# Attention scores: q loaded once and k in both orders of its halves, instead of q in both orders and k once

## The chip, the cores and the metric

The kernel runs on one core of a Trainium2 chip. The metric is the device time of one execution in microseconds (us); times here are medians of several runs. A profile of one execution comes with it, with the span from the first to the last instruction, each engine's instructions and each DMA.

The engines are named as in the profile: PE is the matmul engine TensorE (PEld its weight loads), DVE is VectorE, ACT is ScalarE, POOL is GpSimd, and SP is SyncE, which here only issues DMAs. Every engine runs its own instructions in order.

## The reference, cut to what matters

One transformer layer in float32 over two sequences, a prompt of 1024 tokens and a sample of 512, each with 16 meta tokens ahead. Half of the mixer is grouped-query attention (8 q heads of 64 that share 2 k and v heads), the other half differential attention (4 heads, two softmax maps each).

```
n  = rms_norm(h);  qa, ka, va, qb, kb, vb = split(n @ w_in)
# group A, 8 heads, k and v shared by four
s  = qa . ka / 8 ;  oa = softmax(s) @ va
# group B, 4 heads, maps 0 and 1
s  = qb[c] . kb[c] / 8 ;  a = softmax(s[0]) - lam * softmax(s[1]) ;  ob = rms_norm(a @ vb)
h  = h + concat(oa, ob) @ w_out
n  = rms_norm(h)
h  = h + (gelu(conv3(n @ w_gate)) * (n @ w_up)) @ w_down
y  = rms_norm(h)[16:]
```

q and k of group A are normalised per head, and q and k of both groups are rotated (rotary position).

## The kernel before, in words

**Precision.** A float32 operand is split into hi (rounded to the fast matmul type float32r) and lo (the rest). A dense product is three matmuls: hi hi, hi lo, lo hi (`mm3`, L129 to L131; `split` is L123 and L124). For scores the 64 rows of a head's q stand on the 128 rows of TensorE twice: hi over lo. A k tile holds k's hi over lo. One matmul of q (hi over lo) with k gives hi hi + lo lo, and a second one of q in the other order (lo over hi) gives the two mixed products. Both go to the same PSUM tile (L401 and L402).

**Where q and k come from.** `finish` in the projection writes hi and lo of q and k to DRAM, q as hi, lo, hi so that two neighbours can be read in either order (L237 to L247). `stacked` (L366) reads two neighbours of one head into a 128-row tile, on SP's queue. Its source has four levels: (2 orders x 2 halves) x 32 rows x tokens.

**Tiles.** s is 0 for the prompt (n = 1040 tokens, three pieces of 348 columns for PSUM, so 4 pad columns filled by a second small `stacked`) and 1 for the sample (n = 528, two pieces of 264, no pad). `load_q` takes up to 512 queries, in two tiles, `load_k` a whole k. Pools hold the tiles: `kp` for k, `qp` for q, `pp` for p, and so on; a tile can be loaded again when its last reader is done. A softmax takes up to 128 queries: two matmuls per piece, the scaled copy with its row minimum (L405, DVE), the exponential (L408, ACT), transposes (L422, PE, 128x128), their hi and lo (L123, L124), and the product with v (L432 to L446). In group A the reciprocals of the row sums go through DRAM (`rT`, stored at L454, loaded back at L470); SP waits for the store before it can issue that load. Each of the 4 differential heads has two k (m = 0, 1), a v and three (s = 0) or two (s = 1) blocks of queries; p0 is combined with p1 on POOL (L526, L528). `halo` collects the last meta token's query of four heads.

**Order of the program.** Projection of s = 1 (up to 160 us of the profile); attention of s = 1 merged with the projection of s = 0 (up to about 550 us); attention of s = 0 merged with `mixer_out` and `conv_glu` of s = 1 (up to about 1400 us); `mixer_out` of s = 0 with the rest of that; `conv_glu` of s = 0 (to the end). `merge` interleaves two generators by the work that they report; a scheduler that works with expected durations then sets the order on each engine for the whole program, DMA queues too. So the order moves when a tile's number of buffers or an instruction changes. `mixer_out` (s = 1) begins with h loaded from `oT` (L608, SP), which attention (s = 1) has stored; then its hi (L123, ACT) and the first `mm3`. Weights w_f are loaded on ACT's queue, 512 KB at a time, and split into w_hi and w_lo (L150 on POOL or ACT).

Of the kernel before, what the change touches and what calls it, by code (L numbers as in the profile page):

```python
# [12 lines left out]
F32 = mybir.dt.float32  # L13
F32R = mybir.dt.float32r
# [6 lines left out]
P = 128  # L21
D = 1024
KT = D // P
NMETA = 16
HD = 64
# [10 lines left out]
QA, KA, VA, QB, KB, VB = 0, 4, 5, 6, 10, 14  # L36
# [67 lines left out]
def pool(ctx, g, name, bufs, side):  # L104
    return ctx.enter_context(g.tc.tile_pool(name=name, bufs=bufs, side=side, reuse_waits="tile"))
# [51 lines left out]
def projection(ctx, g, s, side, tag, tag2):  # L157

    nc, tc = g.nc, g.tc
    n = SEQS[s] + NMETA  # L160
# [18 lines left out]
    first = load_weight(g, g.w_in[KA])  # L179

    with tc.tile_pool(name=f"ps{s}", bufs=2, side=side, reuse_waits="tile") as sp:
# [4 lines left out]
        for k in range(KT):  # L186
            x = sp.tile([P, n], F32, name="x", tag="x", bufs=2 if s == 0 else 8)
# [12 lines left out]
        c0, cw = chunks[0]  # L200
        first_ps = g.psum.tile(P, cw, tag)
        dense(g, first_ps, first, xhi, xlo, c0, cw)
        for i, (c0, cw) in enumerate(chunks):
            if s == 1:
                ps = ms[i]
            else:
                ps = g.psum.tile(P, cw, tag2)
# [29 lines left out]
    def finish(y, hn, dst, keys, c0, cw):  # L237

        if hn is not None:
            nc.vector.tensor_tensor(out=y, in0=y, in1=hn[:, None, :].broadcast_to(list(y.shape)), op=ALU.mult)  # L240
        hi = tmp(bp, "hi", y.shape[1], cw, 2, F32R)
        lo = y.bitcast(F32R)
        split(g, hi, lo, y, nc.gpsimd)
        for i, part in enumerate((hi, lo) if keys else (hi, lo, hi)):
            to = dst[i, :, :, c0:c0 + cw]
            to = to.rearrange("x p n -> p x n") if y.shape[1] == 2 else to.rearrange("x p n -> (x p) n")[:, None]
            nc.sync.dma_start(out=to, in_=part.bitcast(F32))  # L247
# [101 lines left out]
def attention(ctx, g, s, side):  # L349
    nc, tc = g.nc, g.tc  # L350
    N = SEQS[s]
    n = N + NMETA

    nch = -(-n // 512)
    kw = -(-n // nch)
    kw += kw % 2
    ne = nch * kw
    nf = n // P
    sp = pool(ctx, g, f"as{s}", 8, side)
    kp = pool(ctx, g, f"ak{s}", 4, side)  # L360
    qp = pool(ctx, g, f"aq{s}", 3 if s == 0 else 2, side)
    vp = pool(ctx, g, f"av{s}", 2, side)
    pp = pool(ctx, g, f"ap{s}", 9 if s == 0 else 6, side)
    ptp = pool(ctx, g, f"apt{s}", 3 if s == 0 else 2, side)
    op = pool(ctx, g, f"ao{s}", 2, side)
    def stacked(tl, j, m, first, c0, cw):  # L366

        src = g.ka[s] if j == KA else g.qk[s][PAIRS.index(j)]
        parts = src[first:first + 2].rearrange("p x (m r) n -> (p x) m r n", r=32)
        nc.sync.dma_start(out=tl.bitcast(F32), in_=parts[:, m, :, c0:c0 + cw])  # L370

    def load_q(j, m, c0, cw):
        out = []
        for first in range(2):
            q = qp.tile([P, 512], F32R, name="q", tag=f"q{first}")[:, :cw]
            stacked(q, j, m, first, c0, cw)
            out.append(q)
        return out

    def load_k(j, m):  # L380
        k = kp.tile([P, ne], F32R, name="k", tag="k")
        stacked(k[:, :n], j, m, 0, 0, n)
        if ne > n:
            stacked(k[:, n:], j, m, 0, 0, ne - n)
        return k

    def load_v(i, w, c0):
        v = vp.tile([P, nf, 2 * P], F32R, name="v", tag="v")[:, :, :w]
# [4 lines left out]

    def softmax(q, k, l):

        M = q[0].shape[-1]
        p = pp.tile([P, ne], F32, name="p", tag="p")[:M]
        ps = g.psum.wide(M, nch, kw)
        for i in range(nch):
            kc = k[:, i * kw:(i + 1) * kw]  # L400
            nc.tensor.matmul(ps[:, i], lhsT=q[0], rhs=kc, start=True, stop=False)  # L401
            g.mark = nc.tensor.matmul(ps[:, i], lhsT=q[1], rhs=kc, start=False, stop=True).ins  # L402

        nm = sp.tile([P, 1], F32, name="nm", tag="nm")[:M]
        nc.vector.tensor_scalar(out=p.rearrange("p (i w) -> p i w", i=nch), in0=ps, scalar1=-HD ** -0.5, scalar2=3.0e38,  # L405
                                op0=ALU.mult, op1=ALU.min, accum_out=nm)
        p = p[:, :n]
        nc.scalar.activation(p, p, AF.Exp, bias=nm, scale=-1.0, accum_out=l)  # L408
        return p
# [46 lines left out]
    def finish_a(o, W):  # L456
        low = op.tile([P, 512], F32, name="o_low", tag="w1", bufs=1)[:HD, :W]
        nc.scalar.copy(low, o[HD:P, :])
        oa = op.tile([P, 512], F32, name="o_a", tag="o", bufs=3)[:HD, :W]
        nc.vector.tensor_tensor(out=oa, in0=o[0:HD, :], in1=low, op=ALU.add)  # L460
        return oa

# [18 lines left out]
    for kv in range(2):  # L481
        k = load_k(KA, kv)
        v = load_v(0, P, kv * P)
        for i in range(4):
            h = kv * 4 + i
            for b in range(nblk):
                q = load_q(QA + 2 * kv, i, NMETA + 512 * b, 512)
                load_r()
                pl = []
                l = sp.tile([P, 4], F32, name="l_a", tag="l_a", bufs=3)  # L490
                for t in range(4):
                    pl.append(softmax([x[:, t * P:(t + 1) * P] for x in q], k, l[:, t:t + 1]))
                    yield 2 * n
                cols = slice(1 + 512 * b, 513 + 512 * b)
                reciprocals(l, g.rT[s][h, cols].rearrange("(t p) -> p t", p=P))
                o, W = yield from weighted_v(pl, v, False)
                oa = finish_a(o, W)
                store_a()
                late.append((oa, g.rT[s][h:h + 1, cols], g.oT[s][h * HD:(h + 1) * HD, cols]))
        halo = [sp.tile([P, 8], F32R, name="halo", tag=f"halo{f}", bufs=2) for f in range(2)]  # L500
        for i in range(4):
            for f in range(2):
                stacked(halo[f][:, 2 * i:2 * i + 2], QA + 2 * kv, i, f, NMETA - 2, 2)
        l = sp.tile([P, 4], F32, name="l_a", tag="l_a", bufs=3)[:8, 0:1]
        load_r()
        p = softmax(halo, k, l)
        r = sp.tile([P, 4], F32, name="r_a", tag="r_a", bufs=3)[:8, 0:1]
        nc.vector.reciprocal(out=r, in_=l)
        nc.scalar.activation(p, p, AF.Copy, scale=r)
        o, W = yield from weighted_v([p], v, False)  # L510
        oa = finish_a(o, W)
        for i in range(4):
            h = kv * 4 + i
            nc.sync.dma_start(out=g.oT[s][h * HD:(h + 1) * HD, 0:1], in_=oa[:, 2 * i + 1:2 * i + 2])
        store_a()

    def diff_block(qs, ks, v, cols):
        pl = []
        for c0, M in cols:
            l = sp.tile([P, 2], F32, name="l_b", tag="l_b")[:M]  # L520
            p0, p1 = [softmax([x[:, c0:c0 + M] for x in qs[m]], ks[m], l[:, m:m + 1]) for m in range(2)]
            r = sp.tile([P, 2], F32, name="r_b", tag="r_b")[:M]
            nc.vector.reciprocal(out=r, in_=l)
            nc.scalar.activation(p0, p0, AF.Copy, scale=r[:, 0:1])
            c = sp.tile([P, 1], F32, name="c", tag="c")[:M]
            nc.gpsimd.tensor_tensor(out=c, in0=r[:, 1:2], in1=g.neglam[:M], op=ALU.mult)  # L526
            nc.scalar.activation(p1, p1, AF.Copy, scale=c)
            nc.gpsimd.tensor_tensor(out=p0, in0=p0, in1=p1, op=ALU.add)  # L528
            pl.append(p0)
            yield 4 * n  # L530
        o, W = yield from weighted_v(pl, v, True)
        ob = op.tile([P, 512], F32, name="o_b", tag="o", bufs=3)[:, :W]
        nc.scalar.copy(ob, o)
        sq = op.tile([P, 512], F32, name="o_sq", tag="w1", bufs=1)[:, :W]
        nc.scalar.activation(sq, ob, AF.Square)
        ms = g.psum.tile(P, W, "o")
        nc.tensor.matmul(ms, lhsT=g.ones_v, rhs=sq, start=True, stop=True)
        rs = op.tile([P, 512], F32, name="o_rs", tag="w1", bufs=1)[:, :W]
        rsqrt_newton(g, op, rs, ms, W)
        nc.vector.scalar_tensor_tensor(out=ob, in0=ob, scalar=g.gsub, in1=rs, op0=ALU.mult, op1=ALU.mult)  # L540
        return ob
# [6 lines left out]
    for h in range(4):  # L548
        ks = [load_k(KB + h // 2 * 2, h % 2 * 2 + m) for m in range(2)]
        v = load_v(1 + h, 2 * P, 0)  # L550
        rows = g.oT[s][512 + h * P:512 + (h + 1) * P]
        for blk in blocks:
            c0 = blk[0][0]
            W = sum(m for _, m in blk)
# [224 lines left out]
def trunk_kernel(ctx, tc, g):  # L779
# [5 lines left out]
    for s, N in enumerate(SEQS):  # L785
        n = N + NMETA
        g.qk.append([dram.tile([3, 2, P, n], F32, name=f"qk{s}_{i}") for i in range(len(PAIRS))])
        g.ka.append(dram.tile([2, 2, HD, n], F32, name=f"ka{s}"))
        g.v.append([dram.tile([P, n // P, 2 * P], F32, name=f"v{s}_{i}") for i in range(5)])

        g.vt.append(dram.tile([5, 96, 2 * P], F32, name=f"vt{s}"))
        g.oT.append(dram.tile([D, N + 1], F32, name=f"oT{s}"))
        g.rT.append(dram.tile([8, N + 1], F32, name=f"rT{s}"))
# [158 lines left out]
```

## Time and profile before

| | us |
|---|---|
| median of 3 runs | 2291.74 |
| the runs | 2291.74, 2292.84, 2283.27 |
| span of the profiled execution | 2286.9 |
| PE busy in it | 2136.4 (93%) |
| PE weight loads busy | 1917.3 (84%) |
| DVE, ACT, POOL busy | 1273.1, 1032.2, 665.6 |

The profiled execution has no time of its own beside its span; the runs, which also hold what lies around the span, are between 3.6 us below and 5.9 us above it. DMA moved 222.76 MB, 97 GB/s in the mean. In the profile, "PE ps_s L401 <- DMA q<-qk" reads: TensorE's instruction at line 401, which writes ps_s, waited for the DMA that fills q from qk. SPq is SP's DMA queue. In a row of a group, busy time and mean length stand before the idle time ahead of it.

### The profile page before, as it was taken

Reading aid. Unit: us, or ns where it says so; the run is one execution under the profiler, and the core shown is the slowest. Engines: PE = TensorE matmul, PEld = TensorE weight load, DVE = VectorE, ACT = ScalarE, POOL = GpSimd, SP = SyncE. Lnnn points to the kernel's source line nnn. Section 1 sums busy time; section 2 is a strip of 40 time slices with the busy share of each in tenths; the row PEclk is TensorE's granted clock in tenths of the full one; section 3 lists DMA queues with packets and bytes.
Section 4 is the critical chain, followed back from the end, with each engine's and each line's share of the span. In section 5 each row is a group of like instructions: output and inputs, shape, how many; then the busy total and the mean of one; then the engine's idle time right before and its main releaser. Section 6 shows DMA issues by size and latency. Waiting matters only on the chain.

```text
span 2286.9 us, 32292 instructions
## 1 busy us (share of the span) xinstructions
PE 2136.4 (93%) x12418; PEld 1917.3 (84%) x12418; DVE 1273.1 (56%) x2203; ACT 1032.2 (45%) x1806; POOL 665.6 (29%) x514
## 2 busy tenths in 40 slices
PE   7888989997599999999999987989999999999997
PEld 6887888996488888888999975988888888888887
DVE  6635544455357666766777774774333444433445
ACT  5434544565346434456777785542122211122224
POOL 5862335442023212124444432431110001111004
PEclk9898999997799999999999997999999999999999
DMA  6564645444533332323333313631111111111112
GB/s 209 172 219 88 140 142 137 161 139 141 120 103 67 93 98 76 87 66 100 110 100 102 106 44 120 202 112 56 37 56 47 47 47 46 43 50 56 46 37 75
DMA packets 126739, 222.76 MB, mean 97 GB/s; under 512 B 28888, under 2 KB 79864, under 8 KB 126072
## 3 DMA queue, kind: packets, MB, share of 16 engines
q1 hardware_dynamic: 97784, 115.82, 17.4%
q10 hardware_dynamic: 28800, 104.87, 15.1%
q8 instruction: 98, 1.61, 0.3%
q14 instruction: 57, 0.47, 0.1%
HBM read 172.10 MB, written 48.55 MB: 96 GB/s over the span
## 4 chain that ended last, share of the span: by engine, by line
PE 67%; DMA 4%; DVE 4%; ACT 2%; issue 1%; SPq 0%; POOL 0%; POOLq 0%; DVEq 0%; ACTq 0%
PE ps_mm L129 17%; PE ps_mm L130 17%; PE ps_mm L131 17%; PE ps_t L422 4%; PE ps_s L401 3%; PE ps_s L402 3%; PE ps_o L437 1%; PE ps_o L436 1%; DMA res<-xT 1%; PE ps_o L432 1%; PE ps_o L434 1%; PE ps_o L433 1%; DMA v<-v 1%; DVE w_lo L124 1%; DMA rT<-r_a 1%
## 5 line engine op out<-in xcount | busy, mean ns | idle before, releaser
L129 PE MATMUL ps_mm<-xhi,w_hi 128*128 128x512 f32 (+6 forms) x1968 | 665.2, 338 | 29.5 <-ACT xhi L123 28.5
L130 PE MATMUL ps_mm<-xlo,w_hi 128*128 128x512 f32 (+6 forms) x1968 | 659.3, 335 | 0.0
L131 PE MATMUL ps_mm<-xhi,w_lo 128*128 128x512 f32 (+6 forms) x1968 | 657.4, 334 | 0.0
L129 PEld LDWEIGHTS ps_mm<-xhi,w_hi 128*128 128x128 f32 x1968 | 374.1, 190 | 54.4 <-ACT xhi L123 28.9
L130 PEld LDWEIGHTS ps_mm<-xlo,w_hi 128*128 128x128 f32 x1968 | 373.5, 190 | 25.0 <-issue 0.9
L131 PEld LDWEIGHTS ps_mm<-xhi,w_lo 128*128 128x128 f32 x1968 | 373.2, 190 | 24.1
L123 ACT CAST w_hi<-w_f 128x1024 fp32r<-128x1024 f32 x134 | 139.4, 1048 | 395.7 <-PE ps_mm L130 357.8
L405 DVE TENSOR_SCALAR_CACHE_REDUCE p<-ps_s 114x1044 f32<-114x1044 f32 (+5 forms) x212 | 223.4, 1054 | 130.3 <-PE ps_s L402 121.0
L124 POOL TENSOR_TENSOR a_lo<-gate,a_hi 128x512 fp32r<-128x512 f32 x66 | 100.3, 1520 | 658.1 <-ACT a_hi L123 654.2
L408 ACT ACTIVATE p<-p,nm 114x1040 f32<-114x1040 f32 (+5 forms) x212 | 215.2, 1015 | 89.3 <-DVE p L405 88.6
L123 ACT CAST pt_hi<-ps_t 128x512 fp32r<-128x512 f32 (+6 forms) x360 | 167.0, 484 | 193.1 <-PE ps_t L422 150.0
L699 DVE TENSOR_TENSOR h<-ps_mm,h 128x512 f32<-128x512 f32 (+1 forms) x288 | 182.1, 645 | 123.4 <-PE ps_mm L131 122.6
L124 DVE TENSOR_TENSOR pt_lo<-ps_t,pt_hi 128x512 fp32r<-128x512 f32 (+4 forms) x312 | 170.6, 563 | 118.0 <-ACT pt_hi L123 117.1
L130 PE MATMUL ps_mm<-a_lo,w_hi 128*128 128x512 f32 (+1 forms) x576 | 216.3, 379 | 0.0
L131 PE MATMUL ps_mm<-a_hi,w_lo 128*128 128x512 f32 (+1 forms) x576 | 215.7, 378 | 0.0
L129 PE MATMUL ps_mm<-a_hi,w_hi 128*128 128x512 f32 (+1 forms) x576 | 214.5, 384 | 0.0
L401 PE MATMUL ps_s<-k,q 128*114 128x348 f32 (+4 forms) x552 | 179.5, 331 | 21.5 <-DMA q<-qk 15.1
L422 PE MATMUL ps_t<-ident,p 128*128 128x128 f32 (+7 forms) x1188 | 187.6, 272 | 9.5 <-ACT p L408 6.2
L402 PE MATMUL ps_s<-k,q 128*114 128x348 f32 (+4 forms) x552 | 173.0, 319 | 10.9 <-DMA q<-qk 10.9
L422 PEld LDWEIGHTS ps_t<-ident,p 128*128 128x128 f32 (+7 forms) x1188 | 143.1, 137 | 41.8 <-issue 9.5
L124 DVE TENSOR_TENSOR w_lo<-w_f,w_hi 128x1024 fp32r<-128x1024 f32 x100 | 122.7, 1236 | 81.8 <-ACT w_hi L123 81.7
L687 DVE TENSOR_TENSOR gate<-ps_mm,gate 128x512 f32<-128x512 f32 x66 | 45.6, 691 | 198.3 <-PE ps_mm L131 195.7
(186 smaller groups left out, 3608.3 us busy)
## 6 DMA issues: line engine op xcount, KB each, us to landing
w_f<-w_gate ACTq DMA_DIRECT2D x44, 512.0 KB
w_f<-w_up ACTq DMA_DIRECT2D x44, 512.0 KB
w_f<-w_down ACTq DMA_DIRECT2D x44, 512.0 KB
w_f<-w_in ACTq DMA_DIRECT2D x36, 512.0 KB
w_f<-w_out ACTq DMA_DIRECT2D x32, 512.0 KB
q<-qk SPq DMA_DIRECT2D x48, 256.0 KB
q<-qk SPq DMA_DIRECT2D x48, 171.0 KB
qk<-hi SPq DMA_DIRECT2D x20, 384.0 KB
```

Of the source, the lines that this page charges most:

```text
L123: nc.scalar.copy(hi, src)
L124: (lo_engine or nc.vector).tensor_tensor(out=lo, in0=src, in1=hi.bitcast(F32), op=ALU.subtract)
L129: nc.tensor.matmul(ps, lhsT=whi, rhs=xhi, start=start, stop=False)
L130: nc.tensor.matmul(ps, lhsT=whi, rhs=xlo, start=False, stop=False)
L131: nc.tensor.matmul(ps, lhsT=wlo, rhs=xhi, start=False, stop=stop)
L401: nc.tensor.matmul(ps[:, i], lhsT=q[0], rhs=kc, start=True, stop=False)
L402: g.mark = nc.tensor.matmul(ps[:, i], lhsT=q[1], rhs=kc, start=False, stop=True).ins
L405: nc.vector.tensor_scalar(out=p.rearrange("p (i w) -> p i w", i=nch), in0=ps, scalar1=-HD ** -0.5, scalar2=3.0e38, op0=ALU.mult, op1=ALU.m ...
L408: nc.scalar.activation(p, p, AF.Exp, bias=nm, scale=-1.0, accum_out=l)
L422: nc.tensor.transpose(tps[:, c:c + M], p[:, k0:k0 + kw], g.ident[:M, :M])
L687: nc.vector.tensor_tensor(out=a, in0=up, in1=a, op=ALU.mult)
L699: nc.vector.tensor_tensor(out=hs, in0=ps, in1=hs, op=ALU.add)
```

## The change

q is stored as hi, lo and k as hi, lo, hi. `load_q` loads one tile (hi over lo) and `load_k` two: hi over lo, and lo over hi. Per piece of scores there are still two matmuls, now with the same q and the two k tiles. The 4 pad columns of each k tile are copied from its first columns on POOL instead of loaded. Buffers: `kp` 3 for each of the two orders instead of 4 in all, `qp` 4 (s = 0) or 3 (s = 1) of one kind instead of 3 or 2 of two kinds, `pp` 8 instead of 9 for s = 0, the o tiles 2 instead of 3 for s = 1, `halo` one tile instead of two.

```
-        for i, part in enumerate((hi, lo) if keys else (hi, lo, hi)):
+        for i, part in enumerate((hi, lo, hi) if keys else (hi, lo)):
...
-    kp = pool(ctx, g, f"ak{s}", 4, side)
-    qp = pool(ctx, g, f"aq{s}", 3 if s == 0 else 2, side)
+    kp = pool(ctx, g, f"ak{s}", 3, side)
+    qp = pool(ctx, g, f"aq{s}", 4 - s, side)
...
-    pp = pool(ctx, g, f"ap{s}", 9 if s == 0 else 6, side)
+    pp = pool(ctx, g, f"ap{s}", 8 if s == 0 else 6, side)
...
     def load_q(j, m, c0, cw):
+        q = qp.tile([P, 512], F32R, name="q", tag="q")[:, :cw]
+        stacked(q, j, m, 0, c0, cw)
+        return q
+
+    def load_k(j, m):
         out = []
         for first in range(2):
-            q = qp.tile([P, 512], F32R, name="q", tag=f"q{first}")[:, :cw]
-            stacked(q, j, m, first, c0, cw)
-            out.append(q)
+            k = kp.tile([P, ne], F32R, name="k", tag=f"k{first}")
+            stacked(k[:, :n], j, m, first, 0, n)
+            if ne > n:
+                nc.gpsimd.tensor_copy(k[:, n:], k[:, :ne - n])
+            out.append(k)
         return out
...
-        M = q[0].shape[-1]
+        M = q.shape[-1]
...
         for i in range(nch):
-            kc = k[:, i * kw:(i + 1) * kw]
-            nc.tensor.matmul(ps[:, i], lhsT=q[0], rhs=kc, start=True, stop=False)
-            g.mark = nc.tensor.matmul(ps[:, i], lhsT=q[1], rhs=kc, start=False, stop=True).ins
+            for first in range(2):
+                g.mark = nc.tensor.matmul(ps[:, i], lhsT=q, rhs=k[first][:, i * kw:(i + 1) * kw],
+                                          start=first == 0, stop=first == 1).ins
...
-        oa = op.tile([P, 512], F32, name="o_a", tag="o", bufs=3)[:HD, :W]
+        oa = op.tile([P, 512], F32, name="o_a", tag="o", bufs=3 - s)[:HD, :W]
...
-        halo = [sp.tile([P, 8], F32R, name="halo", tag=f"halo{f}", bufs=2) for f in range(2)]
+        halo = sp.tile([P, 8], F32R, name="halo", tag="halo", bufs=2)
         for i in range(4):
-            for f in range(2):
-                stacked(halo[f][:, 2 * i:2 * i + 2], QA + 2 * kv, i, f, NMETA - 2, 2)
+            stacked(halo[:, 2 * i:2 * i + 2], QA + 2 * kv, i, 0, NMETA - 2, 2)
...
-        g.ka.append(dram.tile([2, 2, HD, n], F32, name=f"ka{s}"))
+        g.ka.append(dram.tile([3, 2, HD, n], F32, name=f"ka{s}"))
```

In numbers of instructions: 128 q loads become 64, 32 halo loads 16, 20 full k loads 40 (532 KB each for s = 0, 270 KB for s = 1), 10 pad loads become 20 copies on POOL; of the stores of q and k, 20 of q go and 15 of k come. TensorE's matmuls are as many as before.

The order also moves. First SP's queue at the passage from attention of s = 1 to that of s = 0, up to the load of h for `mixer_out` of s = 1. oT_88 and h are of s = 1; ka_66, qk_0 to qk_2, rT_74 are of s = 0; "x2" is two in a row. Before:

```order
L370 DMA halo<-qk_1_61 128x1x2 x6
L370 DMA q<-qk_0_60 128x1x512 x2
L370 DMA halo<-qk_1_61 128x1x2 x2
L370 DMA k<-qk_2_62 128x1x1040
L370 DMA k<-qk_2_62 128x1x4
L454 DMA rT_74<-r_a 128x4x1
L470 DMA o_rb<-rT_74 64x512
L559 DMA oT_88<-o_b 128x306
L608 DMA h<-oT_88 128x513 x8
```

In that piece the two rows of k stand twice, on both sides of the rT store. Now:

```order
L370 DMA halo<-qk_0_60 128x1x2 x4
L370 DMA k<-ka_66 128x1x1040 x2
L389 DMA v<-v_0_67 128x8x128
L391 DMA v_tail<-vt_72 64x128
L370 DMA halo<-qk_1_61 128x1x2 x4
L370 DMA k<-qk_2_62 128x1x1040 x2
L558 DMA oT_88<-o_b 128x306
L607 DMA h<-oT_88 128x513 x8
L617 DMA res<-xT 128x258
```

The rT store and the load at L470 are behind the load of h now, and two full k stand where one stood.

Second, TensorE at the first matmul of `mixer_out` of s = 1 (ps_mm, 128x258). It is number 3130 of TensorE's instructions before, with these around it (p_6045 and q_6775 are of s = 0):

```order
L401 MATMUL ps_s_6783<-k_6033,q_6775 128x348
L402 MATMUL ps_s_6783<-k_6033,q_6777 128x348
L436 MATMUL ps_o_6202<-pt_hi_6380,v_6036 128x512 [waits Activation_49]
L129 MATMUL ps_mm_6109<-xhi_6008,w_hi_6103 128x258 [waits Activation_49]
L129 MATMUL ps_mm_6161<-xhi_6008,w_hi_6103 128x256 [waits Activation_49]
L437 MATMUL ps_o_6202<-pt_lo_6381,v_6036 128x512 [waits DVE_49]
```

Now it is number 3061:

```order
L401 MATMUL ps_s_6147<-k_5990,q_6000 128x348
L401 MATMUL ps_s_6147<-k_5993,q_6000 128x348
L422 MATMUL ps_t_6161<-ident_93,p_6105 128x128 [waits Activation_49]
L422 MATMUL ps_t_6172<-ident_93,p_6105 128x128
L129 MATMUL ps_mm_6067<-xhi_5965,w_hi_6061 128x258 [waits Activation_49]
L401 MATMUL ps_s_6406<-k_5990,q_6400 128x348 [waits DMAHW0_49,DVE_49]
```

Fewer matmuls of attention (s = 0) stand ahead of it: the scores of the second q (q_6400) come after it.

Third, POOL at the border of the first and second differential head of s = 0, at the last combined p of the first head (p_11842 before, p_11757 now). Before:

```order
L526 TENSOR_TENSOR c_11809<-r_b_11806,neglam_131 114x1
L150 CAST w_hi_12486<-w_f_12484 128x1024
L528 TENSOR_TENSOR p_11784<-p_11784,p_11795 114x1040
L526 TENSOR_TENSOR c_11867<-r_b_11864,neglam_131 114x1
L528 TENSOR_TENSOR p_11842<-p_11842,p_11853 114x1040
L150 CAST w_hi_12597<-w_f_12595 128x1024
```

Now (k_11953 and k_11956 are the second head's m = 1 in the two orders, k_12956 the third head's m = 0 in the first):

```order
L383 COPY k_11953<-k_11953 128x4
L527 TENSOR_TENSOR p_11699<-p_11699,p_11710 114x1040
L383 COPY k_11956<-k_11956 128x4
L383 COPY k_12956<-k_12956 128x4
L525 TENSOR_TENSOR c_11782<-r_b_11779,neglam_131 114x1
L150 CAST w_hi_12510<-w_f_12508 128x1024
L527 TENSOR_TENSOR p_11757<-p_11757,p_11768 114x1040
L383 COPY k_12959<-k_12959 128x4
```

Three pad copies, each behind the load of its k, stand ahead of the sum for p_11757; the line numbers of the changed kernel are one lower from here on (L527 is L528 before).

More of the change, by code (lines that the diff above doesn't have):

```diff
@@ L372, in load_q @@
     def load_q(j, m, c0, cw):
+        q = qp.tile([P, 512], F32R, name="q", tag="q")[:, :cw]
+        stacked(q, j, m, 0, c0, cw)
+        return q
+    def load_k(j, m):
         out = []
         for first in range(2):
-            q = qp.tile([P, 512], F32R, name="q", tag=f"q{first}")[:, :cw]
-            stacked(q, j, m, first, c0, cw)
-            out.append(q)
-        return out
[L380 to L385, printed above, removed]
+            k = kp.tile([P, ne], F32R, name="k", tag=f"k{first}")
[3 more added lines that the diff above has]
+            out.append(k)
+        return out
     def load_v(i, w, c0):
@@ L491, in attention @@
                 for t in range(4):
-                    pl.append(softmax([x[:, t * P:(t + 1) * P] for x in q], k, l[:, t:t + 1]))
+                    pl.append(softmax(q[:, t * P:(t + 1) * P], k, l[:, t:t + 1]))
                     yield 2 * n
@@ L520, in diff_block @@
             l = sp.tile([P, 2], F32, name="l_b", tag="l_b")[:M]
-            p0, p1 = [softmax([x[:, c0:c0 + M] for x in qs[m]], ks[m], l[:, m:m + 1]) for m in range(2)]
+            p0, p1 = [softmax(qs[m][:, c0:c0 + M], ks[m], l[:, m:m + 1]) for m in range(2)]
             r = sp.tile([P, 2], F32, name="r_b", tag="r_b")[:M]
@@ L531, in diff_block @@
         o, W = yield from weighted_v(pl, v, True)
-        ob = op.tile([P, 512], F32, name="o_b", tag="o", bufs=3)[:, :W]
+        ob = op.tile([P, 512], F32, name="o_b", tag="o", bufs=3 - s)[:, :W]
         nc.scalar.copy(ob, o)
```

## The prediction

> **What bounds the kernel now.** I read the page first, then the waits of TensorE by stretch, then stretches of time, the chain of waits around the one long idle, and last the issue queue of SyncE (SP), which issues every load of q and k.
>
> ```profile
> span 2286.9 us, 32292 instructions
> PE 2136.4 (93%) x12418; PEld 1917.3 (84%) x12418; DVE 1273.1 (56%) x2203; ACT 1032.2 (45%) x1806; POOL 665.6 (29%) x514
> ```
>
> TensorE (PE) is the bound. It is idle for 2286.9 − 2136.4 = 150 us; the change adds and removes no matmul, so it can act through waits alone. They are not spread evenly. First the waits of TensorE between 160 and 620 us (in total, times, longest), then those between 620 and 1350 us:
>
> ```profile
> PE ps_mm L129 <- ACT xhi L123: 28.5, 1, 28.5
> PE ps_s L401 <- DMA q<-qk: 15.1, 2, 8.1
> PE ps_s L402 <- DMA q<-qk: 10.9, 5, 4.9
> PE ps_t L422 <- ACT p L408: 6.2, 3, 4.1
> ...
> PE ps_s L401 <- DVE p L405: 1.4, 4, 0.7
> PE ps_mm L129 <- DVE h L624: 1.0, 1, 1.0
> ```
>
> Up to 620 us TensorE waits for q, and once 28.5 us for the first xhi of mixer_out(1). After 620 us it waits for nothing over 1.4 us: whatever is added there lengthens the kernel one for one. The stretches below give the price of a matmul, of a cold clock and of a transfer (columns: PE busy and count, weight loads, VectorE, ScalarE, GpSimd, granted clock, mean share of the 16 DMA engines, GB/s).
>
> ```profile
> 355.00:360.00 5.00, 4.51 (x29) 4.05 (x27) 1.23 (x4) 2.20 (x6) 2.41 (x1) 1.00 1.08 133
> 360.00:365.00 5.00, 0.62 (x4) 0.63 (x5) 0.00 (x0) 0.00 (x0) 0.00 (x0) 0.99 0.26 13
> 365.00:370.00 5.00, 5.00 (x21) 4.96 (x21) 2.22 (x4) 1.08 (x2) 0.00 (x0) 0.67 0.69 189
> 370.00:375.00 5.00, 5.00 (x30) 4.46 (x29) 2.56 (x7) 2.06 (x5) 0.66 (x1) 1.00 0.16 58
> ...
> 550.00:555.00 5.00, 4.96 (x18) 4.96 (x19) 2.12 (x4) 1.98 (x4) 0.00 (x0) 0.50 0.26 101
> 575.00:580.00 5.00, 0.00 (x0) 0.00 (x0) 0.00 (x0) 0.00 (x0) 0.00 (x0) 0.99 0.22 68
> 580.00:596.00 16.00, 0.00 (x0) 0.00 (x0) 0.00 (x0) 0.00 (x0) 0.00 (x0) 0.50 0.28 71
> 585.00:590.00 5.00, 0.00 (x0) 0.00 (x0) 0.00 (x0) 0.00 (x0) 0.00 (x0) 0.50 0.25 50
> 595.00:600.00 5.00, 0.00 (x0) 0.00 (x0) 0.00 (x0) 0.00 (x0) 0.00 (x0) 0.50 0.97 237
> 1150.00:1200.00 50.00, 50.00 (x318) 46.08 (x317) 38.84 (x66) 37.75 (x63) 21.33 (x17) 1.00 0.30 95
> 1206.00:1227.00 21.00, 21.00 (x123) 18.84 (x122) 19.14 (x31) 15.41 (x24) 9.65 (x7) 1.00 0.35 116
> ```
>
> Dense matmuls cost 50/318 = 0.158 us each. While only stacked loads (q, k) run, the share stands at 0.25: they occupy four of the sixteen engines, and so go one after another. Four engines moved 50 GB/s at 585 to 590, 71 × 0.25/0.28 = 63 over 580 to 596, 116 × 0.25/0.35 = 83 at 1206 to 1227, and 101 × 0.25/0.26 = 97 at 550 to 555. A k of sequence 0 (128 x 1040 floats, 532 KB) thus takes between 5.5 and 10.6 us, 8.4 in the transition and 6.4 in the saturated part; a q (262 KB) takes 2.7.
>
> The chain around the long idle (start, length, what), then SP's own queue there:
>
> ```profile
> 541.88 8.11 DMA q<-qk
> ...
> 580.67 12.72 DMA rT<-r_a
> 593.41 0.49 SPq L470
> 593.99 0.53 SPq L559
> 594.57 8.34 DMA h<-oT
> 603.00 0.41 ACT xhi L123
> 603.46 0.88 PE ps_mm L129 x2
> ```
>
> ```profile
> 549.16 11.11 SPq L370 DMA_DIRECT2D halo<-qk  x5
> 560.82 1.64 SPq L370 DMA_DIRECT2D halo<-qk  x3
> 568.95 5.66 SPq L370 DMA_DIRECT2D halo<-qk  x6
> 575.87 1.39 SPq L370 DMA_DIRECT2D halo<-qk  x2
> 577.30 3.26 SPq L370 DMA_DIRECT2D k<-qk  x2
> 582.28 3.41 SPq L370 DMA_DIRECT2D k<-qk  x2
> 594.57 8.72 SPq L608 DMA_DIRECT2D h<-oT  x8
> ```
>
> TensorE ran out of work at 575 and waited for h. The chain puts 12.7 us of that on the rT store, which SP waits for before L470. But the two k issued at 577 and 582 would, at 8.4 us each behind what was queued, keep the four engines busy to about 600 anyhow, and h uses those four too; at 595 to 600 the other engines already move (0.97) and still no h has landed. I take the k loads as the limit there.
>
> **The change part by part.**
>
> *Matmuls.* L401 and L402 become one line that runs as often: L401's and L402's 552 + 552 and the halo's. No gain from fewer instructions. What is new is that one q stays the stationary operand for 6 (sequence 1: 4) matmuls in a row. Does that save weight loads?
>
> ```profile
> L129 PEld LDWEIGHTS ps_mm<-xhi,w_hi 128*128 128x128 f32 x1968 | 374.1, 190 | 54.4 <-ACT xhi L123 28.9
> L130 PEld LDWEIGHTS ps_mm<-xlo,w_hi 128*128 128x128 f32 x1968 | 373.5, 190 | 25.0 <-issue 0.9
> ```
>
> L130 uses the w_hi that L129 has just loaded, and its load is there 1968 times at the same 190 ns. So 0. The Trainium skill ("TensorE: Matmul & The Clock Gate", Step-by-step: what each phase is for) says that weights typically stay put over many matmuls, so that one loads once and multiplies repeatedly; the L130 row speaks against that for this code, and the rule is kept below as a rival.
>
> *Bytes.* 64 q loads and 10 pad loads go, 20 k loads come: per k +8.4 or +6.4 us of the four engines, per q −2.7. Over the kernel this nearly cancels; what counts is where they fall.
>
> *Sequence 1's attention (160 to 527 us).* With one q instead of two, the waits at L402 have no cause: −10.9. Of L401's two, the 8.1 us is at the transition (below), the other stays. Against it, the ka stores now stand behind L470 in SP's order and may hold the hi tile and with it ScalarE's p (the 4.1 us wait of L422): between 0 and +8, I take +5. Sum −6. A k of 270 KB takes 2.8 to 5.4 us. With three tiles per order instead of four in all, the second k pair of a head waits for the release of the previous head's first pair; the new order leaves 87, 54 and 65 matmuls from release to first use, at 4.51/29 = 0.156 us 13.6, 8.4 and 10.1 us; two loads and some 1.5 us of issue and landing (an estimate, from SP's half microsecond per issue) need 7.1 to 12.3. Stalls 0 to 6, at 4.1 us per k about 1: +1.
>
> *Transition (527 to 605 us).* Ahead of h, SP now issues 6 full k instead of 4, 4 q instead of 8, 8 halos instead of 16: 2 × 8.4 − 4 × 2.7 = +6; the halos held SP for 19.8 us in all, so half of them gives between 0 and −10, I take −5, and four pad loads and the rT store ahead of h another −1. So h lands at the same time. But of attention(0)'s matmuls, 69 that ran ahead of mixer_out(1)'s first 128x258 matmul (number 3130 of TensorE's order before, 3061 now) come after it: 69 × 0.158 = 10.9 us of cover that TensorE now spends idle and has to do later. Sum +11. Ends: with k at 5.5 us and −10, +0; with 10.6 us and no gain from halos, +21; and if the chain is right and SP's wait is the limit, 12.7 lower, −2 at my middle.
>
> *Saturated part (620 to 1350).* Differential head h+1's second pair of k may load only when head h's first pair is released. From release to first use lie 107, 68 and 101 matmuls: 16.9, 10.7 and 16.0 us. The pair needs 2 × 6.4 + 1.5 = 14.3: stalls 0, 3.6, 0. Second, the pad copy. GpSimd runs in order, and its copies for the pair and for the next k stand ahead of the last p sum of head h, which TensorE wants 143 matmuls (22.6 us) after the release. Three loads, a q between (1.7) and the sum itself (2.4) come to 3 × 6.4 + 1.5 + 1.7 + 2.4 = 24.8: stall 2.2 at the first border; at the second (144 matmuls) the 3.6 covers it. The copies themselves are priced by the nearest small row:
>
> ```profile
> L526 POOL TENSOR_TENSOR c<-r_b,neglam x56: 184/190/1163, 376.2 to 1375.1; 114x1 f32<-114x1 f32 x36, 102x1 f32<-102x1 f32 x12, 104x1 f32<-104x1 f32 x8
> L528 POOL TENSOR_TENSOR p<-p x56: 1296/2432/3484, 378.9 to 1376.8; 114x1040 f32<-114x1040 f32 x36, 102x528 f32<-102x528 f32 x12, 104x528 f32<-104x528 f32 x8
> SPq L370 <- PE ps_s L402: 263.0, 42, 27.6
> ```
>
> 20 × 0.19 = 4 us on an engine that is busy 29%: nothing. The last row shows that SP already waits up to 27.6 us for TensorE to release a tile; with fewer tiles everything queued behind such a wait is later, o's stores and the next q among it. A stall also cools the clock: after the 4.9 us without q at 360 to 365 the next 5 us held 21 matmuls against 30 after it, 9 × 0.167 = 1.5 us. One such stall: +1.5. Sum 3.6 + 2.2 + 1.5 = +7. Ends: at 5.5 us per k +2, at 10.6 about +36. The Trainium skill ("TensorE: Matmul & The Clock Gate", What's actually happening) lets the clock fall only after about 3.4 us of idleness; by it the 2.2 us stall stays warm, as taken here, and if both stalls cooled the clock the sum would be 1.5 higher.
>
> *After 1350 us* the order on TensorE is the same in both, and attention is over: 0. Fewer tiles of p (8 for 9) and o: 0, since TensorE waits for DVE's p at most 1.4 us in the saturated part; ends 0 and +4.
>
> Sum: −6 + 1 + 11 + 7 = **+13 us**. The profiled execution's span of 2286.9 plus what lies around it stands for the median of 2291.7 (runs 2283.3 to 2292.8), so 2305.
>
> **Rivals.** *Faster.* SP's wait for rT is what held h, as the chain says: the new order has L470 behind h. Then the transition gives −2, or −8 with k at 5.5 us; k of the saturated part comes in time (5.5 us: +2), and −6 stays: −6 as a whole; with k at 5.5 throughout, the halos' whole −10 and no loss to the ka stores −8 − 5 + 2 − 11 = −22. The middle is −14. It decides if h lands before about 590. For it: the 12.72 row. Against it: four engines busy without a break from 575 to 596. About 2278.
>
> *Weights stay.* If repeated stationary q were not reloaded, 912 loads go (138 softmaxes of sequence 0 × 5, 74 of sequence 1 × 3). Loads are busy 46.08/317 = 0.145 us of each matmul's 0.158, so at most some 0.016 us of each matmul could open up, an estimate: −15 against the sum, 2290. Against it: the L130 row.
>
> *No change that can be measured.* The change moves no net bytes off the four engines, and its gain at q and its losses at k cancel: k at 7 us and the halos' whole 10 us in the transition (+3), saturated part +3, −6 + 1 as above: +1, 2293.
>
> *Much slower.* k at 8.4 us in the saturated part too: pair 18.3, stalls 1.4, 7.6 and 2.3; p at the first border 30.8 − 22.6 − 1.4 = 6.8; two or three cold clocks +4: +22 instead of +7, 2320; worse if ScalarE's weight loads wait behind the k on the same engines.
>
> **How the numbers follow.** 0.5% of 2291.7, 11.5 us, is about what a measurement of this kernel can tell from no change: 2280.3 to 2303.2. Chances: the forecast with k as priced 0.34 (2298 to 2313, two thirds above the bound), much slower 0.25, cancelled 0.20, faster 0.17, weights 0.04 (within the bound). Slower 0.34 × 0.65 + 0.25 = 0.47; faster 0.17; same the rest, 0.36. The range leaves out a tenth on each side: from 2277 (the faster rival's middle) to 2326 (the much slower one with the transition at its upper part).
>
> **What would show it.** Right: no wait at the second matmul for q; the wait of mixer_out(1)'s first matmul near 40 us instead of 28.5; new TensorE waits for k or for GpSimd's p at the two or three borders between differential heads, 2 to 8 us each; weight loads still one per matmul. Wrong: h landing near 590 and a wait there under 25 us (SP's rT wait was the limit), k landing within 5.5 us, or a share well over 0.25 while k loads alone run.

## The result, and the profile after

The changed kernel takes 2318.59 us (median of 4 runs, 2314.45 to 2319.85) against 2290.18 us before: a ratio of 1.0115, 95% interval 1.0101 to 1.0130. It is slower, as forecast; the difference is twice what the sum gave (28 us for 13).

First the page: the span and the share of each engine.

```profile
span 2318.1 us, 32190 instructions
PE 2136.3 (92%) x12418; PEld 1917.2 (83%) x12418; DVE 1281.7 (55%) x2203; ACT 1033.3 (45%) x1806; POOL 663.0 (29%) x534
```

TensorE's busy time and count are those of before, so the 31.2 us more of span are, in sum, all idle time of TensorE; within single stretches its busy time moves too, with the clock. To place them I took the same four points of TensorE's work in both traces: the first score matmul of sequence 0, the first matmul of `mixer_out` (sequence 1), its 401st score matmul (within the first softmax of the differential heads), and its last one.

| stretch of TensorE's work | before, us | after, us | difference |
|---|---|---|---|
| start to first scores of sequence 0 | 547.5 | 539.8 | −7.7 |
| to the first matmul of `mixer_out` | 55.9 | 44.5 | −11.4 |
| to the differential heads | 428.1 | 435.4 | +7.3 |
| differential heads | 337.8 | 380.1 | +42.3 |
| to the end | 917.5 | 918.2 | about +1 |

The loss is in the differential heads. That stretch as one window, first before, then after (same columns as in the prediction):

```profile
1031.60:1369.50 337.90, 332.59 (x2080) 302.24 (x2079) 256.16 (x450) 259.00 (x425) 142.25 (x109) 1.00 0.30 94
```

```profile
1019.70:1399.80 380.10, 347.70 (x2083) 311.18 (x2082) 258.02 (x450) 258.85 (x423) 140.59 (x122) 0.96 0.26 84
```

As many matmuls (2080 and 2083) were busy 15.1 us longer (the mean clock is 0.96, not 1.00), and TensorE was idle 32.4 us instead of 5.3. Where those stalls come from stands in the chain of waits after, which enters the DMA of a k once at each of four borders: from group A to the first differential head (at 1016), and between the four heads. These are the longest pieces of the chain there:

```profile
1016.67 17.95 DMA k<-qk
...
1116.44 19.06 DMA k<-qk
1135.99 1.16 ACT p L526
1137.60 1.15 ACT p L408 x2
...
1217.07 20.45 DMA k<-qk
...
1315.45 17.23 DMA k<-qk
1333.17 1.16 ACT p L526
```

Yet TensorE itself hardly waits for k. Its waits between 620 and 1410 us after:

```profile
PE ps_s L401 <- DVE p L405: 12.3, 12, 2.8
PE ps_mm L129 <- ACT p L408: 7.0, 1, 7.0
PE ps_o L432 <- ACT pt_hi L123: 5.6, 2, 4.5
...
PE ps_s L401 <- DMA k<-qk: 3.5, 3, 1.9
```

It waits for ScalarE and VectorE; even a conv_glu matmul (L129), which has nothing to do with k, waits 7.0 us for ScalarE. The link is GpSimd, at 1111 to 1143 us (start, length, what, idle time before and its releaser):

```profile
1121.90 0.19 POOL L383 CAST k<-k 128x4 fp32r<-128x4 f32 x1 [10.60 <-DMA k<-qk]
1122.05 2.43 POOL L527 TENSOR_TENSOR p<-p 114x1040 f32<-114x1040 f32 x1
1128.23 0.19 POOL L383 CAST k<-k 128x4 fp32r<-128x4 f32 x1 [3.75 <-DMA k<-qk]
1135.62 0.19 POOL L383 CAST k<-k 128x4 fp32r<-128x4 f32 x1 [7.20 <-DMA k<-qk]
1135.76 0.19 POOL L525 TENSOR_TENSOR c<-r_b,neglam 114x1 f32<-114x1 f32 x1
```

and what ScalarE did in that time, then one of its waits over 1000 to 1400 us (in total, times, longest):

```profile
1119.71 1.17 ACT L523 ACTIVATE p<-p,r_b 114x1040 f32<-114x1040 f32 x1
1135.99 1.16 ACT L526 ACTIVATE p<-p,c 114x1040 f32<-114x1040 f32 x1 [15.10 <-POOL c L525]
```

```profile
ACT p L526 <- POOL c L525: 39.4, 4, 15.1
```

A pad copy waits on GpSimd for its k. Behind it stands c = r times −lambda, one column of 0.19 us. ScalarE's next instruction needs c and stops for 15.1 us; behind that stand the exponential of the next scores, the hi casts and the gelu of conv_glu. One slow load stops four engines, through an instruction of 0.19 us. In the kernel before, ScalarE has no wait for c in that stretch (the same instruction is at L527 there).

### The profile page after: what moved, and what is told of

Same layout as the page of the kernel before. It is cut to its first block, busy times and chain, and to the rows that moved or that the text cites. A ratio compares the mean times of both kernels' runs of the same rounds, so it can differ in the third digit from the quotient of the medians.

```text
span 2318.1 us, 32190 instructions
## 1 busy us (share of the span) xinstructions
PE 2136.3 (92%) x12418; PEld 1917.2 (83%) x12418; DVE 1281.7 (55%) x2203; ACT 1033.3 (45%) x1806; POOL 663.0 (29%) x534
## 4 chain that ended last, share of the span: by engine, by line
PE 75%; DMA 10%; DVE 6%; ACT 3%; SPq 3%; issue 2%; POOL 1%; ACTq 0%; POOLq 0%; DVEq 0%
PE ps_mm L129 18%; PE ps_mm L130 18%; PE ps_mm L131 18%; PE ps_s L401 6%; PE ps_t L422 4%; DMA k<-qk 3%; SPq L370 2%; DMA v<-v 2%; DMA rT<-r_a 1%; PE ps_o L437 1%; PE ps_o L436 1%; DMA h<-oT 1%; PE ps_p L129 1%; PE ps_p L131 1%; PE ps_p L130 1%
## 5 line engine op out<-in xcount | busy, mean ns | idle before, releaser
L129 PE MATMUL ps_mm<-xhi,w_hi 128*128 128x512 f32 (+6 forms) x1968 | 664.8, 338 | 39.4 <-ACT xhi L123 31.6
L129 PEld LDWEIGHTS ps_mm<-xhi,w_hi 128*128 128x128 f32 x1968 | 374.7, 190 | 64.2 <-ACT xhi L123 32.0
L401 PE MATMUL ps_s<-k,q 128*114 128x348 f32 (+4 forms) x1104 | 223.1, 328 | 46.9 <-DMA q<-qk 28.4
L401 PEld LDWEIGHTS ps_s<-k,q 128*128 128x128 f32 (+3 forms) x1104 | 176.0, 186 | 62.8 <-issue 30.1
L129 PE MATMUL ps_mm<-a_hi,w_hi 128*128 128x512 f32 (+1 forms) x576 | 216.3, 387 | 0.0
```

The costliest lines, as they stand in the source:

```text
L129: nc.tensor.matmul(ps, lhsT=whi, rhs=xhi, start=start, stop=False)
L401: g.mark = nc.tensor.matmul(ps[:, i], lhsT=q, rhs=k[first][:, i * kw:(i + 1) * kw], start=first == 0, stop=first == 1).ins
```

## The experiments

Each was timed in 3 rounds beside the kernel before on the same chip (medians of before 2278.6 to 2281.3 us there). The ratios have 95% intervals; "heads" is the stretch of the differential heads (before 337.8, after 380.1). The scheduler makes a new order for each kernel, so differences of a few us between them also hold moved instructions.

**Pads loaded by DMA again.**

```
-                nc.gpsimd.tensor_copy(k[:, n:], k[:, :ne - n])
+                stacked(k[:, n:], j, m, first, 0, ne - n)
```

> The changed kernel with the 4 pad columns of each k tile loaded by a small DMA again instead of copied on GpSimd; all else as in the change. Theory P (the copies on GpSimd wait for the k loads, and what is queued behind them on GpSimd, the p sums, o_a and weight casts, then starves TensorE): the stretch from the 400th to the last score matmul group of sequence 0 falls from 380 us to about 345 to 350 and the time to about 2285 to 2290. Rival B (three tiles per order, so k is loaded too late and the scores themselves wait): the stretch stays above 370, the waits just move to L401, about 2312. Rival C (twice the bytes of k on four engines): as B.

2311.4 us, ratio 1.0124 (1.0104 to 1.0145); heads 368.9. My theory of the copies fell short here: 11 us of the stretch came back and the time did not move measurably against the change. Taken alone this would have spoken for the rivals. But it is no clean removal: ScalarE's wait for c is indeed gone (0.2 us instead of 39.4), yet TensorE's order in the heads is another one here, with only 14% of its matmuls at the same place as in the change.

**No pad step in attention.** The DRAM tiles of k hold 4 columns more, stored once by the projection:

```
+            if keys and c0 == 0 and dst.shape[-1] > n:
+                to = dst[i, :, :, n:]
...
+                nc.sync.dma_start(out=to, in_=part[:, :, :dst.shape[-1] - n].bitcast(F32))
...
-            stacked(k[:, :n], j, m, first, 0, n)
-            if ne > n:
-                nc.gpsimd.tensor_copy(k[:, n:], k[:, :ne - n])
+            stacked(k, j, m, first, 0, ne)
```

> The changed kernel without any pad step in attention: the projection stores the 4 pad columns once behind each k in DRAM (15 small stores more in sequence 0), and each k tile is one load of 1044 columns. Theory P: about 2280 to 2288, a little below the run with pad loads, since 20 small loads fewer stand in SyncE's queue. Rivals B and C: about 2310. If the small loads cost nothing the two runs agree within 3 us.

2289.4 us, ratio 1.0034 (1.0022 to 1.0047); heads 355.0. TensorE's order in the heads is that of the change, matmul for matmul, so this is the clean removal: without the copies the stretch is 25.1 us shorter, and the row of ScalarE's wait for c is gone from its larger waits. What is left against before is 17 us, with TensorE now waiting for k itself at the borders (from 620 to 1400 us):

```profile
PE ps_s L403 <- DMA k<-qk: 9.3, 3, 3.8
```

The 22 us between pad loads and no pads were not expected from that run. With pad loads the clock was lower at the borders (0.74 and 0.83 in stretches of 20 us at two of them, 0.91 and 0.91 without); that they delay the q and k behind them is likely, but with the other order it was not isolated.

**Only the copies, in the kernel before.**

```
-            stacked(k[:, n:], j, m, 0, 0, ne - n)
+            nc.gpsimd.tensor_copy(k[:, n:], k[:, :ne - n])
```

> The kernel before (q in both orders, k once, 4 tiles of k) with only the pad columns copied on GpSimd: 10 copies. Theory P: the copies hold GpSimd here too, but each k was requested a head ahead and lands in half the time, so TensorE loses less than in the change: 3 to 15 us over before, with GpSimd waits named k <- DMA k<-qk. Rivals B and C: no change, within 3 us of before.

2317.6 us, ratio 1.0152 (1.0130 to 1.0174): ten copies of 0.19 us, with q, k and their buffers as they were, cost 36 us, more than the whole change and more than I expected. Heads 365.5, +27.7. These k are not even due: with four tiles, the two that are loaded at a border are for the head after next, but their copies already stand in GpSimd's order, ahead of c. ScalarE waits for it (1000 to 1410 us):

```profile
ACT p L527 <- POOL c L526: 31.5, 4, 14.7
```

GpSimd's wait for k in that stretch, in this run and after the change:

```profile
POOL k L384 <- DMA k<-qk: 42.3, 4, 16.0
```

```profile
POOL k L383 <- DMA k<-qk: 71.2, 11, 13.9
```

So the copies alone are enough, and they cost about the same 25 to 28 us in the heads in either layout. TensorE's order is that of before here, but for 9% of its matmuls in the heads.

**Four tiles per order of k.**

```
-    kp = pool(ctx, g, f"ak{s}", 3, side)
-    qp = pool(ctx, g, f"aq{s}", 4 - s, side)
+    kp = pool(ctx, g, f"ak{s}", 4 - s, side)
+    qp = pool(ctx, g, f"aq{s}", 2 + s, side)
...
-    pp = pool(ctx, g, f"ap{s}", 8 if s == 0 else 6, side)
+    pp = pool(ctx, g, f"ap{s}", 7 if s == 0 else 6, side)
```

> The changed kernel with 4 instead of 3 tiles per order of k for sequence 0; to make room p has 7 tiles instead of 8 and q 2 instead of 4 there. Rival B: k is requested a head ahead, the waits at the borders go, about 2285 to 2290, if the fewer tiles of p and q cost nothing. Theory P: the copies still stand ahead of the p sums, but k lands before GpSimd comes to them, so most of the loss goes as well (about 2290 to 2300); the run tells apart only whether an early k is enough. Rival C: still over 2305.

2343.6 us, ratio 1.0269 (1.0249 to 1.0288); heads 398.2. Rival B and theory P missed; rival C's "over 2305" holds only in the letter, since C has no reason for 25 us more than the change. The same edit on top of the pads in DRAM:

> The change with pads in DRAM and 4 tiles per order of k, 7 of p and 2 of q for sequence 0 (as in the earlier run with 4 tiles of k, but without copies on GpSimd). Theory P: that run's 2344 came from the copies and, in part, from fewer tiles of p and q, so this one falls by 25 us or more. Rival B: with the release out of the way the stretch of the differential heads falls to about 340; if it stays at 355 or more, fewer tiles of p and q cost as much as the fourth k gives.

2329.4 us, ratio 1.0212 (1.0190 to 1.0233); heads 375.6. It fell by 14 us only, and TensorE now waits for q (160 to 1400 us; 19.9 of it in the heads, where the run with four q tiles has no such wait):

```profile
PE ps_s L403 <- DMA q<-qk: 46.5, 6, 14.3
```

Two q tiles are too few; what a fourth k is worth stays open, since both runs that have it have fewer tiles of q and p.

**Pads in DRAM, in the kernel before.** The same storing of pads, with the pad load dropped.

> The kernel before with its pad columns stored in DRAM by the projection: 10 small loads fewer in attention, no copy on GpSimd. Theory P with an open price of the small loads: with pad loads the change was 22 us slower than with pads in DRAM; if a small load behind each k costs by itself, this run is 3 to 10 us faster than before; if that price came only from the tight k loads of the change, it is within 3 us of before.

2279.4 us, ratio 1.0000 (0.9987 to 1.0013). A small load behind a k that was requested a head ahead costs nothing that can be measured.

**No wait for rT, in the kernel before.**

```
-                late.append((oa, g.rT[s][h:h + 1, cols], g.oT[s][h * HD:(h + 1) * HD, cols]))
+                late.append((oa, g.rope_in[0, 0:1, cols], g.oT[s][h * HD:(h + 1) * HD, cols]))
```

> The kernel before, with the row-sum factors of group A loaded from a constant table instead of from the rT store (the normalisation of group A is left out of the computation in this way), so SyncE no longer waits there. Theory of the prediction (the queued k loads, not the wait for rT, hold h): the first matmul of mixer_out(1) waits 25 to 30 us as before. Rival (the wait for rT holds h): the wait falls by about 12 us, to 14 to 18.

2274.5 us, ratio 0.9977 (0.9964 to 0.9990). TensorE's order is that of before, and the wait at `mixer_out` did not shorten, although the chain before had put 12.7 us of it on rT (the load of h waits 7.0 us for a k in SP's queue instead):

```profile
PE ps_mm L129 <- ACT xhi L123: 30.8, 1, 30.8
```

**k on all sixteen engines.** In the source of `stacked` the outermost level, order by half, has 4 entries of 32 rows each. Here k is loaded as four DMAs of 32 rows each, on top of the pads in DRAM:

```
-        nc.sync.dma_start(out=tl.bitcast(F32), in_=parts[:, m, :, c0:c0 + cw])
+        for a in range(4 if cw > 512 else 1):
+            w = slice(a * 32, a * 32 + 32) if cw > 512 else slice(0, P)
+            nc.sync.dma_start(out=tl[w].bitcast(F32), in_=parts[a, m, :, c0:c0 + cw] if cw > 512 else parts[:, m, :, c0:c0 + cw])
```

> The change with pads in DRAM, and each k tile loaded by four DMAs of 32 rows instead of one whose source has four levels. If the slowest level of the source (4) is what holds a k to four engines, the share while k loads rises well over 0.25 and a k takes 2 to 4 us. Rival C (the transfer of twice the k is what remains of the loss): the stretch of the differential heads falls from 355 to about 340, h lands earlier, the time is 2260 to 2278. Rival B (release of the tiles): the first k of a pair still comes late, the stretch stays over 350, about 2285.

2253.7 us, ratio 0.9880 (0.9858 to 0.9902): 36 us below the run without the split, and below both kernels. Heads 342.4, so of the 17 us that were left 13 went with the split; the tiles are as many as before the split, so their release was not the limit. TensorE's order is another one than without the split (11% of its matmuls in the heads at the same place), so the 13 us need not be the transfer time alone. Around the loads of the first k and q of sequence 0 the share is no longer 0.25:

```profile
517.00:524.00 7.00, 3.35 (x14) 1.93 (x11) 2.39 (x7) 4.75 (x12) 3.31 (x4) 0.51 0.95 281
```

The Trainium skill ("DMA: Bandwidth & Descriptors", Why a DMA increments its semaphore by 16 and not by 1) says that a DMA is spread over the largest number up to 16 that divides the slowest dimension of both sides; for 4 and 128 that is 4, for 32 and 32 it is 16, and the shares of 0.25 and 0.95 agree. The 0.95 holds loads of v, q and w_f as well, so the semaphores in the traces, the counters by which a DMA reports that it landed, are the better witness: an unsplit k is counted up four times as it lands (in the changed kernel, the one issued at 1314.82 us: 10.2, 10.6, 11.5 and 11.7 us later), each split quarter 16 times. And behind two unsplit q, 12 of a quarter's 16 counts came within 6.4 us (issued at 1086.99 us here), the other four only at 9.8 to 10.4 us. At that border the first k was complete 5.0 us after its first issue, against 10.9 us in the changed kernel.

**Split k, with the copies on GpSimd kept.** The same three lines in the changed kernel.

> The changed kernel with its copies on GpSimd, and only each k load split into four DMAs of 32 rows. Theory P in its refined form (a copy costs because it waits in GpSimd's order for a slow k): with a k in 3 to 5 us the copies wait little, so the time is within 10 us of the split run without copies (2254), under 2265, and GpSimd's waits for k fall from 71 us to under 25 in the differential heads. Rival (a copy on GpSimd costs in itself, through its place in the order): it keeps the 25 us, about 2279.

2253.8 us, ratio 0.9884 (0.9869 to 0.9898): the same time as without copies. GpSimd's wait for k in the heads, which theory P had put under 25:

```profile
POOL k L385 <- DMA k<-qk: 32.1, 8, 7.6
```

The heads are 355.3 here, 13 us longer than without copies, in the same order of TensorE, and ScalarE still waits 6.8 us for c. So a copy is not free, but with a fast k its 25 us are halved. The parts ahead of the heads were 14 us shorter, in the same order too, and why was not traced, so that the two times are equal is not explained.

**k and q split, in both layouts.** As the split of k, for every load wider than the halo's two columns:

```
-        for a in range(4 if cw > 512 else 1):
+        for a in range(4 if cw > 2 else 1):
```

> The change with pads in DRAM and both k and q loads split into four DMAs. If the four engines are what q waits for, the q waits of sequence 1's attention (10.6 us at its start, 13.0 us at the start of sequence 0 without any split) shrink and the time falls below 2254, to 2235 to 2250; if SyncE's issue of some half microsecond per DMA binds, it stays at 2254 or rises to 2265.

> The kernel before (q in both orders, k once) with pads in DRAM and each k load split into four DMAs. It tells what the exchange of q for k is worth where a k is fast. If the change's saved q loads are a gain once k is cheap, this run is 5 to 20 us slower than the change with split k (2254), at 2260 to 2274; if not, within 4 us of it or faster.

> The kernel before with pads in DRAM and both q and k loads split into four DMAs. If the exchange of q for k acts only through the four engines, this run and the change with both split agree within 5 us; if the 64 q loads more, now 256 DMAs on SyncE, cost issue time, it is 5 to 20 us slower.

| pads in DRAM and | q in both orders, k once (before) | q once, k in both orders (the change) |
|---|---|---|
| no split | 2279.4, 1.0000 (0.9987 to 1.0013) | 2289.4, 1.0034 (1.0022 to 1.0047) |
| k split | 2265.9, 0.9938 (0.9918 to 0.9958) | 2253.7, 0.9880 (0.9858 to 0.9902) |
| k and q split | 2252.8, 0.9876 (0.9860 to 0.9893) | 2228.8, 0.9772 (0.9758 to 0.9787) |

The sign of the exchange turns with the price of a k: a loss of 8 to 10 us on four engines, a gain of 12 with k split and of 24 with both split. With k split the gain lies ahead of the heads, which begin at 995.5 instead of 1011.6 us; the heads themselves take 342.4 against 337.9. With both split they begin at 972.4 instead of 990.0 us and take 341.9 against 351.9. The run with both split was faster than forecast, and 24 us is more than the 5 to 20 named for 256 DMAs on SyncE; how much of it is issue time was not isolated. The last is the best version found, 51 us (2.3%) below before on its chip.

## Why the prediction was right or wrong

**Right: where and by what.** A wait in the saturated part lengthens the kernel one for one; the loss came at the borders of the differential heads, through k loads and GpSimd's copies. The gain on q, which should have paid for part of it, did not come (below), and the signs named for the borders are not what the trace shows: TensorE's waits for k are 3.5 us in all, none over 1.9, and its stalls there are put down to ScalarE and VectorE. TensorE loads weights as often as before, one load per matmul at 180 ns although q stays, so that rival is out:

```profile
L401 PEld LDWEIGHTS ps_s<-k,q x1104: 164/180/338, 168.7 to 1399.7; 128*128 128x128 f32 x86, 128*114 128x114 f32 x72, 128*102 128x102 f32 x16, 128*104 128x104 f32 x10
```

**Mis-sized: the saturated part, +7 for +42.** It ended beyond even the upper end of 36. The loads were slower than priced: from a pair's first issue to the copy of its second k it took 16.3 to 18.7 us at the four borders (after 1110.91, for example, at 1128.23) against 14.3, and three loads with a q between, 22.4 without the sum, came to 24.7 (issued from 1110.9, third copy at 1135.6). The failed step is what stands behind the copies. I priced the last p sum, which TensorE wants 22.6 us after the release, and so found 2.2 us. I had shown the row of c and read it as the price of a copy only. c stands behind the copies too, and ScalarE waits for it at the head of its own order, so the stall began when ScalarE had its next p ready, not when TensorE needed the last one, and it took conv_glu along. Removing the copies gave 25.1 of the 42.3; the rest, 17.2, is put down to the late pair: 13 of it went with the split of k, in another order, so this part is likely and not shown.

**Mis-sized: the cold clock, +1.5 for +15.1** (347.70 − 332.59), since TensorE stalled at four borders, not one, for 4 to 9 us in all at each, and ran at a lower clock after it. The rule that the prediction cites from the Trainium skill ("TensorE: Matmul & The Clock Gate", What's actually happening), that the clock falls only after some 3.4 us of idleness, does not hold here; half of that is enough. In the kernel before TensorE was busy for 1.78 of 3.4 us, and in the next 3.4 us the granted clock was 0.51:

```profile
1368.35:1371.75 3.40, 1.78 (x12) 1.42 (x11) 2.32 (x7) 3.40 (x7) 0.19 (x1) 1.00 0.01 2
1371.75:1375.15 3.40, 1.72 (x5) 0.71 (x4) 0.17 (x1) 3.40 (x5) 2.41 (x2) 0.51 0.00 0
```

So the stall of 2.2 us, taken as warm, would not have been safe either.

**Wrong sign: the transition, +11 for −4** (−11.4 + 7.3). The 69 matmuls did move behind h. But h came 19 us earlier in the trace (584.28 instead of 603.46 for the first matmul), half of it (9.4) because the first k of sequence 0 was issued at 515.99 instead of 525.36, which I had not counted, and half because the queue from there to h ran 10 us shorter than before, where I had forecast the same length; which of its terms (k at 8.4 us, halos at −5) was wrong was not separated. The wait at that matmul was 31.6 us, neither near the 40 of the forecast nor under 25. The limit itself was read rightly: with the rT wait gone the first matmul of `mixer_out` came 57.1 us after the first scores of sequence 0 (55.9 before), and with k on sixteen engines its wait fell. In the layout of before with pads in DRAM, without and with the split of k:

```profile
PE ps_mm L129 <- ACT xhi L123: 31.9, 1, 31.9
```

```profile
PE ps_mm L129 <- ACT xhi L123: 20.8, 1, 20.8
```

**The first part, −5 for −7.7: nearly the number, not the step.** The waits at the second matmul for q are gone, as said. But those at the first matmul grew from 15.1 us to 28.4 (160 to 620 us, after):

```profile
PE ps_s L401 <- DMA q<-qk: 28.4, 4, 12.9
```

With the 10.9 at the second matmul, TensorE had waited 26.0 us for q before; so the wait moved and did not shrink. The wait for p grew from 6.2 to 11.0 us, +4.8 where I had taken +5. Up to the first scores of sequence 0 TensorE was idle for 71.7 us in both kernels. The 7.7 us are busy time, 468.1 us instead of 475.8; two runs that leave TensorE's order there as before (pads in DRAM, no rT wait) have 469.3 and 470.9, so the change need not be the cause, and that the number came out was luck.

**The sum.** Forecast were −5, +11, +7 and 0, measured −7.7, −4, +42 and +1. Two misses of opposite sign, −15 in the transition and +35 in the heads, cancel in part; that the time lies well inside the range owes something to that.

**The rivals.** "Faster" fell with the rT run, "weights stay" with the row above, "no change" with the time. "Much slower" had the time (2320) and the price of a k right: 18.3 us for a pair, where 16.3 to 18.7 were measured. Its +22 for the saturated part still was half of what came, since it too went by the last p sum and not by c, and its +11 for the transition made up for that.

**Slips in the working.** 50/318 is 0.157 and not 0.158; 0.158 − 0.145 is 0.013 and not 0.016, so "weights stay" would give −12 instead of −15; the upper end of the transition adds up to +20, not +21; and the 8.1 us wait for q, placed at the transition, is at the start of sequence 1's attention, while the one at the transition is 7.0. None moves the forecast.

## What to carry to other kernels

Before moving a small operation to an engine that seems idle, list what stands behind it in that engine's order and who waits for that: 10 copies of 0.19 us cost 36 us, 28 of them in the differential heads, because they wait for a load ahead of a one-column product that ScalarE needs. Price a load by the share of DMA engines at which it runs; a share of 0.25 while only it runs says that the access pattern, not the memory, sets its time, and here repairing that gained more than any exchange of loads. An exchange of loads judged while loads are slow may come out with the other sign once they are fast, so the bottleneck comes first.

## What the runs showed of the hardware that was not expected

A load of k issued as one DMA ran at a share of 0.25 and took 17 to 20 us from issue to landing where others were queued before it; issued as four DMAs of a quarter each, one was complete 5.0 us after its first issue. Four borders with 4 to 9 us of idleness each, within 380 us, lowered the mean granted clock to 0.96 and cost 15.1 us of busy time on as many matmuls, on top of 27.1 us of added idleness; 1.6 us of idleness within 3.4 us were enough to halve the clock. And a releaser in the chain need not be the limit: taking away the 12.7 us wait that the chain named left the wait behind it at 30.8 us, against 28.5 before.
